# Seven products for thirteen more pairs of row blocks in an fp32 encoder layer

## The chip, the core and the metric

The kernel runs on one core of one Trainium2 chip. The metric is the device time of one execution in microseconds (us). A core has a matrix engine (TensorE, "PE" in the profile, its weight loads "PEld"), VectorE ("DVE"), ScalarE ("ACT"), GpSimd ("POOL") and SyncE ("SP"), which here issues the weight DMAs. Each engine works off its own instructions in order; engines wait for one another by semaphores.

## The reference

One encoder layer on 256 tokens of width 4096, all in float32:

- `h = rms_norm(x)`, then `proj = h @ w_in`, cut into latents for one attention (MLA: 16 heads, with rotary keys), its gate (2048 columns), q, k, v of a second, dilated attention (2048 columns each) and its gate (2048).
- MLA: q from `c_q @ w_uq`, k and v from `c_kv @ w_ukv`, softmax, output; the dilated attention likewise with a distance penalty and three patterns.
- Each output is RMS-normalised and multiplied by `silu(gate)`; then `x = x + concat(y_a, y_b) @ w_out`.
- `x = x + (p @ w_ple) * sigmoid(rms_norm(x) @ w_ple_gate)`, then a last RMS norm.

Nearly all the work is in products of 256 rows with weight matrices of 4096 rows: `w_in`, `w_out` and `w_ple_gate`.

## The kernel before

**Split numbers.** TensorE reads float32 in a rounded form (fp32r). Each operand is therefore cut into a high part (`hi`, rounded by ScalarE, L115 or L829) and a low part (`lo = x - hi`, by VectorE, L116 or L832), and a product is three matmuls (`mm`, L130: L133 hi x hi, L134 the activations' hi x the weights' lo, L135 lo x hi). The activations are split once; every weight tile is split as it arrives.

**Steps.** The kernel is one list `steps`. A step loads a weight tile of 128x1024 (L790, on SP's queue), splits it into a pair of tiles `hi`, `lo`, and runs its matmuls. "Half" below means such a split tile, "lead" the time between the end of its low part and the first matmul that reads it. The main loop (L1430) writes for each step: the loads some steps ahead, the splits some steps ahead (`convert`, as far as tiles are open), the step's matmuls, and then one tick (`advance`, L240) of all running tasks (attention heads, gating, sums). So what lies on VectorE behind what is fixed by this loop, and a split can only be written for a step if the tiles' last user is a step whose matmuls are already written (`tiles`, L1353). The tiles are the ring `WP` of three pairs plus those which a block's `ring` adds from memory that is free then; with one added there are four open, with two five. A ring entry in `gated_rings` (L1194) opens when its flag is set.

**Blocks.** `Block` (L765) multiplies all 256 rows by 1024 columns. It has 32 row blocks of the weights, in 16 pairs. A plain pair ("C" in the strings) takes two steps of four products, that is 2 x 4 x 3 = 24 matmuls of 128x512. A fast pair ("S", `fast_steps`, L808) computes the same 2x2 block product with seven products (Winograd's form of Strassen's scheme): 21 matmuls in four steps of 3, 6, 6 and 6. It needs sums of the activations, made once per pair index by `add_sums` (L848: five operations and a split), and four 128x512 subtractions of weights on VectorE, and its two loads give four split operands of 512, 1024, 1024 and 1024 columns. The seven products lie in eight PSUM banks (m0 to m3, s, o, t0, t1), named by `tags`. When the last fast pair has run, a task (`mid`) combines products; at the block's end another (`done`) adds the rest: in q, k, v these are five operations on L669 (`d_mid`) and four on L687 (`d_done`). The strings in `mix(...)` fix the order; `mix` gives the S the first pair indices.

**Order of the work.** Stage A: the first 1600 columns of `w_in` (400 at a time), while x is transposed. Then "first gates" (block of two latent-gate chunks), then ga2 (third gate chunk) interleaved with `w_uq` and `w_ukv` and the MLA heads (`attend`, L386); `done_uk` (L498) reads the two banks of each `w_ukv` product. Then ga3 (fourth gate chunk), the blocks q0, k0, v0, q1, k1, v1, the four gate chunks of the dilated branch (with its heads), three blocks of `w_out` (o0, o1, o2) and two plain chunks, three blocks of `w_ple_gate` (w0, w1, w2, each with two steps "e" of `w_ple`), and a tail.

**Sums.** `x0_sums` (hook at step 24) serves the first gates, `x_sums` q to v, `y_sums` the `w_out` blocks, and `x1_sums` (spawned six steps into the last plain `w_out` chunk) the `w_ple_gate` blocks. Their results lie in slots such as T0 to T7 and B0 to B7b, which are used again and again by name; a new tile in a slot waits until its last reader is done.

Of the kernel before, what the change touches and what calls it, by code (L numbers as in the profile page):

```python
# [12 lines left out]
F32R = mybir.dt.float32r  # L13
# [5 lines left out]
P = 128  # L19
S = 256  # L20
# [58 lines left out]
def encoder_layer(ctx: ExitStack, tc: tile.TileContext, x, p, positions, g_mix, w_in, g_q_latent, w_uq,  # L79
# [3 lines left out]
    x, p, out = x[0], p[0, 0], out[0]  # L83
    w_in, w_uq, w_ukv, w_out, w_ple, w_ple_gate = (w[0] for w in (w_in, w_uq, w_ukv, w_out, w_ple, w_ple_gate))
# [220 lines left out]
    T7 = {}  # L305

    sums = stat(NT * 6).rearrange("p (c t) -> p c t", t=NT)
# [162 lines left out]
    pairs = {}  # L470
# [58 lines left out]
    us, yT = {}, {}  # L529
# [172 lines left out]
    x1T = {}  # L702
# [49 lines left out]
    WP = ["wp"] * 3  # L752

    class Step:
# [4 lines left out]
        def __init__(self, load, split, run, needs=(), frees=0):  # L759
            self.load, self.split, self.run, self.needs, self.frees, self.after = load, split, run, needs, frees, None  # L760
            self.ring = WP
# [3 lines left out]
    class Block:  # L765
# [6 lines left out]

        NAMES = "M2", "X", "M3", "M4", "M1", "M5", "M6", "M7"

        def __init__(self, w, lhs, sums, name, order, needs, tags, tmp, ring):
            self.w, self.lhs, self.sums, self.name, self.needs, self.tmp = w, lhs, sums, name, needs, tmp
            self.ring, self.tags = ring, dict(zip(self.NAMES, tags))
            self.ps, self.left = {}, {}
            for kind, _ in order:
                for m in ("M1", "M5", "M7", "M6", "M4", "M2", "M3") if kind == "fast" else ("M2", "X", "M3", "M4"):  # L780
                    self.left[m] = self.left.get(m, 0) + (1 if kind == "fast" else 2)
# [66 lines left out]
    def add_sums(n, pair, dst, tmp, name, out, rest=0, first=0):  # L848

        def task():
            def two(op, d, a, b):
                nc.vector.tensor_tensor(d, a, b, op=op)

            if isinstance(tmp, tuple):
                w = [slot(b, [8, P]) for b in tmp]
            else:
                both = slot(tmp, [2, 8, P])
                w = [both[:, 0], both[:, 1]]  # L860
            for j in range(first, n):
# [12 lines left out]
                for _ in range(1 + rest):  # L874
                    yield
        return task()


    y_s, zy = {}, {}
    WIDE_O, FAST_O = 3, 6  # L880
# [7 lines left out]
    def y_sums():  # L888
        while not all(("yT", 0, c) in flags for c in range(FAST_O // 2)):
            yield  # L890
        yield from add_sums(FAST_O, lambda j: [q[:, 2 * (j % 2):2 * (j % 2) + 2] for q in yT[j // 2]], zy_dst, "Al1",
                            "y_sums", y_s)

    def out_mid(k, blk):
        def task():
# [35 lines left out]
    pT, ple, gF, U = [], {}, [], []  # L931
    part2 = [stat(1) for _ in range(NT)]
    blocks = [(512 * c, 512) for c in range(7)] + [(3584, 256), (3840, 256)]
    FAST, WIDE = 6, 3
    zs = {}

    def z_dst(j):
        if j == 0:
            whole = slot("B0", [2, 2 * Q], F32R)
            pT.append(whole[:, 0].rearrange("p (a k t) -> p a k t", a=2, k=2))  # L940
            zs[0] = whole[:, 1].rearrange("p (a i c) -> p a i c", a=2, i=4)
        elif j in (1, 3):
            both = slot(f"B{2 + j // 2}", [2, 2, 4, P], F32R)
            zs[j], zs[j + 1] = both[:, 0], both[:, 1]
        elif j == 5:
            zs[5] = slot("B7a", [2, 4, P], F32R)
            rest = slot("T6", [2, Q])
            P4[1, 0], P4[1, 1] = rest[:, 0], rest[:, 1]
        return zs[j]

    def lhs_x1(kt):
# [173 lines left out]
    M = ("m0", "m1"), ("m2", "m3")  # L1125
# [20 lines left out]
    EVEN, ODD = ("m0", "m1", "s", "o", "m2", "m3", "t0", "t1"), ("m2", "m3", "t0", "t1", "m0", "m1", "s", "o")  # L1146
    LAST = "m2", "m3", "s", "o", "m0", "m1", "t0", "t1"

    def mix(shape):
        n = shape.count("S")  # L1150
        fast, plain_ = iter(range(n)), iter(range(n, 16))
        return [("ple", 0) if x == "e" else ("fast", next(fast)) if x == "S" else ("plain", next(plain_)) for x in shape]

    def lay(blk, order, mid, done, ple=None):
        last = max(i for i, o in enumerate(order) if o[0] == "fast")
        for i, (kind, j) in enumerate(order):
            if kind == "fast":
                new = blk.fast_steps(j)
            elif kind == "ple":
                new = ple  # L1160
            else:
                new = [x for kt in (2 * j, 2 * j + 1) for x in blk.plain_step(kt)]
            if i == last:
                new[-1].after = mid
            if i == len(order) - 1:
                new[-1].after = done
            for x in new:
                x.ring = blk.ring
            steps.extend(new)

    def hook(at, f):
        assert at not in hooks
        hooks[at] = f
# [6 lines left out]
    x0_s, z0 = {}, {}  # L1180

    def z0_dst(j):
        if j < 4:
            if j % 2 == 0:
                both = slot(("B2", "B3")[j // 2], [2, 2, 4, P], F32R)
                z0[j], z0[j + 1] = both[:, 0], both[:, 1]
            return z0[j]
        return slot(f"T{j - 4}", [2, 4, P], F32R)

    def x_pair(j):  # L1190
        return [q[:, 2 * (j % 4):2 * (j % 4) + 2] for q in xT[j // 4]]

    hook(24, lambda: spawn(add_sums(6, x_pair, z0_dst, ("B7a", "B7b"), "x0_sums", x0_s, 2)))
    gated_rings = {("T4", "T7"): ("mid", ("k", 1)), "Al1": ("y_sums", FAST_O - 1), ("T5", "T6"): "kpe"}  # L1194
    order = mix("CCCCSCSCSCSCSCSC")
    blk = Block(w_in[:, OFF_GA:OFF_GA + 1024], lhs_x, x0_s, "x0_sums", order, lambda kt: (), LAST, ("T2", "T3"),
                WP + [("T5", "T6")])
    lay(blk, order, gates_mid(blk), gates_done(blk))
# [7 lines left out]
    hook(len(steps), lambda: spawn(y_stats(0)))  # L1206
    hook(len(steps) + 1, lambda: spawn(x_sums()))
    ga3 = from_x(OFF_GA + 1536, 512, done_gate(0, 3))
    ga3.banks = M[1]
    add(ga3)  # L1210

    x_s = {}
# [10 lines left out]

    for n, key in enumerate((key, i) for i in range(2) for key in "qkv"):
        off = {"q": OFF_Q, "k": OFF_K, "v": OFF_V}[key[0]] + 1024 * key[1]
        order = mix(("CCCCCCCCSCSCSCSC", "CCSCSCSCSCSCSCSC", "CSCSCSCSCSCSCSSC", "CCCCSCSCSCSCSCSC", "CCCCSCSCSCSCSCSC",
                     "CCCCCSCCSCCSCCSC")[n])
        ring = (["B6"], ["B4", "B6"], ["B4", "B6"], ["B4", "B1"], ["B1"], [("T4", "T7")])[n]
        blk = Block(w_in[:, off:off + 1024], lhs_x, x_s, "x_sums", order, lambda kt: (), (EVEN, ODD)[n % 2],
                    "B1" if n < 3 else ("T5", "T6"), WP + ring)  # L1230
        lay(blk, order, d_mid(key, blk), d_done(key, blk))
    beside = [len(steps), len(steps) + 64]
    for c in range(4):
# [6 lines left out]
    for k in range(WIDE_O):  # L1240
        hook(len(steps), only(*(("t0", "t1"), ("m0", "m1"), ("m2", "m3"))[k]))
        for h in range(2):
            hook(len(steps) + 4 + h, lambda c=2 * k + h: load_res(c))
        order = mix(("CCCCCCSCSCSCSCCC", "CCCSCSCSCSCSCSCC", "CCCSCCSCCSCCSCCC")[k])
        blk = Block(w_out[:, 1024 * k:1024 * (k + 1)], lhs_y, y_s, "y_sums", order, lambda kt: need_y(kt // 2),
                    (EVEN, ODD)[k % 2], "Al2" if k < 2 else "Al1", WP + (["Ah2", "Al1"] if k < 2 else [("B7b", "T7")]))
        lay(blk, order, out_mid(k, blk), out_done(k, blk))
# [11 lines left out]
                     lambda j: ["pT"])  # L1259

    for k in range(WIDE):
        order = mix("CCCSCSCSCSCSCSCeC")
        blk = Block(w_ple_gate[:, 1024 * k:1024 * (k + 1)], lhs_x1, x1_s, "x1_sums", [o for o in order if o[0] != "ple"],
                    lambda kt: [("x1T", kt // 4)], LAST, "B6", WP + ["B4", "B5"])
        lay(blk, order, wide_mid(k, blk), wide_done(k, blk), wide_ple(k))
    wide_end = len(steps)
    hooks[wide_end + 2] = lambda: (load_g(0), load_g(1), spawn(late_gains()))
# [2 lines left out]
    for c, (lo, n) in enumerate(blocks):  # L1270
        if c < 2 * WIDE:
            continue
        w, per = cols(w_ple_gate, lo, n), 1024 // n
# [156 lines left out]
    for i, step in enumerate(steps):  # L1430
# [23 lines left out]
        n = 0  # L1454
# [33 lines left out]
```

## Time and profile before

| | us |
|---|---|
| median of 3 runs (lowest, highest) | 1938.94 (1937.89, 1939.36) |
| the profiled execution, whole | 1939.64 |
| its span, first to last instruction | 1937.7 |
| DVE `lo` of 128x1024 (L116), mean of one | 1.223 |
| ACT `hi` of 128x1024 (L115), mean of one | 1.060 |
| DVE subtraction of 128x512 (L816), mean of one | 0.690 |
| load of 512 KB of `w_in`, issue to landing, median | 4.0 |

The profile is one execution. Its first lines give each engine's busy time; the chain is the work that ended last, followed back; "L133 <- DVE B L119" means that the instruction of line 133 waited until VectorE's instruction of line 119 that writes a tile B was done. A matmul's duration in a row is pipelined, so the rate is read from starts, not from durations. A table by stretches has, per row, the stretch, its length, busy time of PE, PEld, DVE, ACT and POOL with the number of instructions in brackets, the granted TensorE clock as a share of the full one, the DMA engines' busy share and GB/s. A timeline row has start, duration, engine, line, operation, `out<-in`, shapes, and in square brackets the idle time before it and who ended it.

### The profile page before, as it was taken

The page shows a single profiled execution, that of the slowest core. Times are in us where ns is not written, and L with a number is a line of the kernel's source. Part 1 is how long each engine was busy: PE and PEld are TensorE (multiplying, and loading weights), DVE is VectorE, ACT ScalarE, POOL GpSimd, SP SyncE. Part 2 cuts the span into 40 slices and gives each one's busy share as a digit, 9 for nine tenths or more (in the row PEclk, how much of TensorE's full clock was granted, in tenths as well). Part 3 has the DMA queues.
Part 4 walks back from the last instruction along what each step waited for, and adds up shares of the span by engine and source line. Part 5 has one row for each costly group of instructions (what it writes and reads, how often), then busy time and mean ns, then how long its engine had stood idle before and what let it go on. Part 6 is the DMA issues. An engine that isn't in the chain of part 4 may idle for free.

```text
span 1937.7 us, 25517 instructions
## 1 busy us (share of the span) xinstructions
PE 1919.8 (99%) x9314; PEld 1636.6 (84%) x9314; DVE 1497.8 (77%) x2071; ACT 1082.0 (56%) x1482; POOL 72.1 (4%) x124
## 2 busy tenths in 40 slices
PE   9999999999999999999999999999999999999997
PEld 8998889997888888888888888888888888888887
DVE  7767966665889988878677777888876598888765
ACT  6555565564555555545456676556555455655543
POOL 1001011110000000000000010000000000000000
PEclk9999999999999999999999999999999999999999
DMA  7666655444656566666654446665666556566655
GB/s 251 190 184 196 196 170 149 145 146 148 188 177 211 196 217 197 216 191 200 215 189 143 149 152 217 220 215 176 205 194 212 187 187 218 191 218 206 225 185 178
DMA packets 146477, 370.58 MB, mean 191 GB/s; under 512 B 11924, under 2 KB 45808, under 8 KB 146096
## 3 DMA queue, kind: packets, MB, share of 16 engines
q1 hardware_dynamic: 144432, 361.80, 58.5%
q0 software_dynamic: 1920, 7.15, 1.1%
q8 instruction: 73, 1.20, 0.2%
q14 instruction: 52, 0.43, 0.1%
HBM read 364.72 MB, written 4.19 MB: 190 GB/s over the span
## 4 chain that ended last, share of the span: by engine, by line
PE 95%; DVE 3%; ACT 1%; issue 1%; DMA 1%; SPq 0%; DVEq 0%; ACTq 0%
PE m L134 20%; PE m L133 20%; PE m L135 20%; PE t L133 4%; PE t L135 4%; PE t L134 4%; PE o L134 3%; PE o L135 3%; PE o L133 3%; PE s L134 3%; PE s L133 3%; PE s L135 3%; DVE lo L116 1%; PE t L443 1%; PE t L393 0%
## 5 line engine op out<-in xcount | busy, mean ns | idle before, releaser
L116 DVE TENSOR_TENSOR lo<-raw,hi 128x1024 fp32r<-128x1024 f32 (+4 forms) x503 | 560.3, 1122 | 239.4 <-ACT hi L115 238.0
L115 ACT ACTIVATE hi<-raw 128x1024 fp32r<-128x1024 f32 (+4 forms) x503 | 488.1, 979 | 333.1 <-PE m L135 137.8
L133 PE MATMUL m<-hi,Ah 128*128 128x512 f32 (+2 forms) x1122 | 426.9, 381 | 2.7 <-DVE B L119 2.7
L134 PE MATMUL m<-lo,Ah 128*128 128x512 f32 (+2 forms) x1122 | 421.7, 376 | 1.0 <-DVE lo L832 0.5
L135 PE MATMUL m<-hi,Al 128*128 128x512 f32 (+2 forms) x1118 | 419.1, 375 | 0.0
L133 PEld LDWEIGHTS m<-hi,Ah 128*128 128x128 f32 x1122 | 211.8, 189 | 32.8 <-issue 3.3
L134 PEld LDWEIGHTS m<-lo,Ah 128*128 128x128 f32 x1122 | 211.9, 189 | 32.6 <-DVE lo L116 2.2
L135 PEld LDWEIGHTS m<-hi,Al 128*128 128x128 f32 x1118 | 211.0, 189 | 32.9 <-DVE Al L127 0.2
L133 PE MATMUL m<-hi,B 128*128 128x512 f32 (+1 forms) x405 | 154.6, 382 | 0.0
L135 PE MATMUL m<-hi,B 128*128 128x512 f32 (+1 forms) x405 | 150.9, 373 | 0.0
L134 PE MATMUL m<-lo,B 128*128 128x512 f32 (+1 forms) x405 | 150.8, 372 | 0.0
L116 DVE TENSOR_TENSOR B<-raw,B 128x1024 fp32r<-128x1024 f32 (+1 forms) x72 | 79.6, 1118 | 26.3 <-ACT B L115 26.3
L115 ACT ACTIVATE B<-raw 128x1024 fp32r<-128x1024 f32 (+1 forms) x72 | 69.2, 975 | 44.6 <-PE o L135 15.6
L135 PEld LDWEIGHTS m<-hi,B 128*128 128x128 f32 x405 | 76.0, 188 | 11.2
L134 PEld LDWEIGHTS m<-lo,B 128*128 128x128 f32 x405 | 76.2, 188 | 10.2 <-DVE lo L116 0.2
L133 PEld LDWEIGHTS m<-hi,B 128*128 128x128 f32 x405 | 76.1, 188 | 10.0
L116 DVE TENSOR_TENSOR T<-t,T 128x512 fp32r<-128x512 f32 (+1 forms) x65 | 44.5, 685 | 41.7 <-ACT T L115 41.4
L829 ACT ACTIVATE hi<-raw 128x1024 fp32r<-128x1024 f32 x45 | 47.9, 1064 | 44.2 <-PE o L135 17.6
L115 ACT ACTIVATE hi<-B 128x1024 fp32r<-128x1024 f32 x42 | 44.7, 1064 | 41.2 <-PE o L135 28.1
L115 ACT ACTIVATE hi<-T 128x1024 fp32r<-128x1024 f32 x34 | 36.2, 1063 | 52.6 <-PE o L135 28.6
L133 PE MATMUL m<-B,Ah 128*128 128x512 f32 (+1 forms) x174 | 64.5, 371 | 0.0
L135 PE MATMUL m<-B,Al 128*128 128x512 f32 (+1 forms) x174 | 64.3, 370 | 0.0
(751 smaller groups left out, 3827.6 us busy)
## 6 DMA issues: line engine op xcount, KB each, us to landing
raw<-in_w_in_dram SPq DMA_DIRECT2D x320, 512.0 KB, 4.0
raw<-in_w_out_dram SPq DMA_DIRECT2D x128, 512.0 KB, 4.4
raw<-in_w_ple_gate_dram SPq DMA_DIRECT2D x128, 512.0 KB, 4.6
raw<-in_w_in_dram SPq DMA_DIRECT2D x63, 400.0 KB, 3.2
raw<-in_w_uq_dram SPq DMA_DIRECT2D x32, 384.0 KB, 3.4
raw<-in_w_ukv_dram SPq DMA_DIRECT2D x16, 512.0 KB, 4.1
T<-in_x_dram SPq DMA_DIRECT2D x7, 512.0 KB, 5.8
T<-in_x_dram POOLq DMA_DIRECT2D x7, 512.0 KB, 8.0
```

What stands on the lines that cost most here:

```text
L115: nc.scalar.activation(hi, src, AF.Copy)
L116: nc.vector.tensor_tensor(lo, src, plain(hi), op=ALU.subtract)
L133: nc.tensor.matmul(ps, ah, bh, start=start, stop=False)
L134: nc.tensor.matmul(ps, ah, bl, start=False, stop=False)
L135: nc.tensor.matmul(ps, al, bh, start=False, stop=stop)
L443: nc.tensor.transpose(tp[:, k, t * P:(t + 1) * P], e[:, t, k * P:(k + 1) * P], ident)
L829: nc.scalar.activation(hi, r[1], AF.Copy)
```

## The change

Three things change.

1. **More fast pairs**, 86 in place of 73: first gates 6 to 7; k0 7 to 8; q1 and k1 6 to 8; v1 4 to 6 (pair indices 0 to 3, 6 and 7, as T4 and T7 become split tiles in this block); o1 6 to 7; o2 4 to 6; w1 and w2 6 to 7. q0 (4), v0 (8), o0 (4) and w0 (6) stay. Strings move with it: k0, q1 and k1 now have v0's "CSCSCSCSCSCSCSSC".
2. **What the sums need.** x0, y and x1 sums are made for seven pairs instead of six. The seventh x0 sum takes B7a (the sums' scratch moves to T2, T3), the seventh y sum T4, the seventh x1 sum B5, which leaves the ring of the `w_ple_gate` blocks. Because q1 to v1 use pairs 6 and 7, T5 and T6 hold sums there, so the subtractions' scratch is B1, and B1 leaves the rings of q1 and k1. In k1 the last four entries of the string ("CSSC") use `WP` alone (`spare`), since B4 receives k1's result.
3. **Banks.** ga3 takes m0, m1 in place of m2, m3; q0 and k0 get other bank orders to fit.

```
-        yield from add_sums(FAST_O, lambda j: [...yT[j // 2]], zy_dst, "Al1", "y_sums", y_s)
+        pair = lambda j: [q[:, 2 * (j % 2):2 * (j % 2) + 2] for q in yT[j // 2]]
+        yield from add_sums(FAST_O, pair, zy_dst, "Al1", "y_sums", y_s)
+        while ("yT", 1, 3) not in flags:
+            yield
+        yield from add_sums(FAST_O + 1, pair, lambda j: slot("T4", [2, 4, P], F32R), ("T7", "B7b"), "y_sums", y_s, first=FAST_O)
...
-    FAST, WIDE = 6, 3
+    FAST, WIDE = 7, 3
...
+        elif j == 6:
+            zs[6] = slot("B5", [2, 4, P], F32R)
...
-    def mix(shape):
-        n = shape.count("S")
-        fast, plain_ = iter(range(n)), iter(range(n, 16))
+    def mix(shape, pairs=range(16)):
+
+        chosen = list(pairs)[:shape.count("S")]
+        fast, plain_ = iter(chosen), iter(j for j in range(16) if j not in chosen)
...
-                x.ring = blk.ring
+                x.ring = blk.ring if i < len(order) - blk.spare else WP
...
-        return slot(f"T{j - 4}", [2, 4, P], F32R)
+        return slot(("T0", "T1", "B7a")[j - 4], [2, 4, P], F32R)
...
-    hook(24, lambda: spawn(add_sums(6, x_pair, z0_dst, ("B7a", "B7b"), "x0_sums", x0_s, 2)))
+    hook(24, lambda: spawn(add_sums(7, x_pair, z0_dst, ("T2", "T3"), "x0_sums", x0_s, 2)))
...
-    order = mix("CCCCSCSCSCSCSCSC")
+    order = mix("CCSCSCSCSCSCSCSC")
...
-    ga3.banks = M[1]
+    ga3.banks = M[0]
...
-        order = mix(("CCCCCCCCSCSCSCSC", "CCSCSCSCSCSCSCSC", "CSCSCSCSCSCSCSSC", "CCCCSCSCSCSCSCSC", "CCCCSCSCSCSCSCSC",
-                     "CCCCCSCCSCCSCCSC")[n])
-        ring = (["B6"], ["B4", "B6"], ["B4", "B6"], ["B4", "B1"], ["B1"], [("T4", "T7")])[n]
-        blk = Block(w_in[:, off:off + 1024], lhs_x, x_s, "x_sums", order, lambda kt: (), (EVEN, ODD)[n % 2],
-                    "B1" if n < 3 else ("T5", "T6"), WP + ring)
+        full = "CSCSCSCSCSCSCSSC"
+        order = mix("CCCCCCCCSCSCSCSC") if n == 0 else mix(full) if n < 5 else mix("CCCCSCSCSCSCSCSC", (0, 1, 2, 3, 6, 7))
+        ring = (["B6"], ["B4", "B6"], ["B4", "B6"], ["B4"], ["B4"], [("T4", "T7")])[n]
+        tags = LAST if n == 0 else ("t0", "t1", "m2", "m3", "m0", "m1", "s", "o") if n == 1 else (EVEN, ODD)[n % 2]
+        blk = Block(w_in[:, off:off + 1024], lhs_x, x_s, "x_sums", order, lambda kt: (), tags, "B1", WP + ring,
+                    4 if n == 4 else 0)
...
-        order = mix(("CCCCCCSCSCSCSCCC", "CCCSCSCSCSCSCSCC", "CCCSCCSCCSCCSCCC")[k])
+        order = mix(("CCCCCCSCSCSCSCCC", "CCSCSCSCSCSCSSCC", "CCCSCSCSCSCSCSCC")[k])
...
-        order = mix("CCCSCSCSCSCSCSCeC")
+        order = mix("CCCSCSCSCSCSCSCeC" if k == 0 else "CCSCSCSCSCSCSSCeC")
...
-                    lambda kt: [("x1T", kt // 4)], LAST, "B6", WP + ["B4", "B5"])
+                    lambda kt: [("x1T", kt // 4)], LAST, "B6", WP + ["B4"])
```

More of the change, by code (lines that the diff above doesn't have):

```diff
@@ L773, in encoder_layer, with __init__ @@
         NAMES = "M2", "X", "M3", "M4", "M1", "M5", "M6", "M7"
-        def __init__(self, w, lhs, sums, name, order, needs, tags, tmp, ring):
+        def __init__(self, w, lhs, sums, name, order, needs, tags, tmp, ring, spare=0):
             self.w, self.lhs, self.sums, self.name, self.needs, self.tmp = w, lhs, sums, name, needs, tmp
+            self.spare = spare
             self.ring, self.tags = ring, dict(zip(self.NAMES, tags))
@@ L890, in y_sums @@
             yield
-        yield from add_sums(FAST_O, lambda j: [q[:, 2 * (j % 2):2 * (j % 2) + 2] for q in yT[j // 2]], zy_dst, "Al1",
-                            "y_sums", y_s)
+        pair = lambda j: [q[:, 2 * (j % 2):2 * (j % 2) + 2] for q in yT[j // 2]]
[3 more added lines that the diff above has]
+        yield from add_sums(FAST_O + 1, pair, lambda j: slot("T4", [2, 4, P], F32R), ("T7", "B7b"), "y_sums", y_s, first=FAST_O)
     def out_mid(k, blk):
```

## The prediction

> **What bounds the kernel now.** I read the busy shares first, then the chain that ended last, TensorE's waits, the table by stretches (one per block of products), and last the timeline around the places that change.
>
> ```profile
> PE 1919.8 (99%) x9314; PEld 1636.6 (84%) x9314; DVE 1497.8 (77%) x2071; ACT 1082.0 (56%) x1482; POOL 72.1 (4%) x124
> ...
> PE 95%; DVE 3%; ACT 1%; issue 1%; DMA 1%; SPq 0%; DVEq 0%; ACTq 0%
> ```
>
> TensorE is the bound: it is 95% of the chain, so a matmul less is worth its start-to-start time unless something else is then late. That time comes from a block without gaps: k1 (832.39 to 915.35 us) issues 366 matmuls of 512 columns in 82.96 us, 0.227 us each; the row's 0.39 us is pipelined latency. A plain pair (24 matmuls) takes 5.44 us, a pair by seven products (21) 4.76. VectorE is what could be late. Back to back its operations start 1.135 us apart (128x1024) and 0.602 us apart (128x512). A plain pair costs it two of the first, 2.27 us; a seven-product pair four subtractions, one short and three long low halves, 6.41 us: 1.65 us more than TensorE's 4.76.
>
> ```profile
> 667.80:749.40 81.60, 81.60 (x361) 67.59 (x360) 76.16 (x89) 47.98 (x50) 0.00 (x0) 1.00 0.64 206
> 749.40:832.40 83.00, 83.00 (x368) 68.72 (x367) 69.31 (x78) 43.40 (x45) 0.00 (x0) 1.00 0.63 203
> 832.40:915.30 82.90, 82.90 (x367) 68.70 (x366) 67.56 (x77) 45.30 (x47) 0.00 (x0) 1.00 0.61 197
> ```
>
> These stretches are v0 (eight fast pairs), q1 and k1 (six each); the columns are stretch, PE, PEld, DVE, ACT and POOL busy, clock, DMA. Eight pairs fill VectorE to 93% and TensorE has no gap. So capacity suffices on the average, and the question is the lead: how long a low half is finished (L116, L832) before the first matmul that reads it (L134).
>
> **What goes.** 13 pairs change, three matmuls each: 39 x 0.227 = **8.85 us less**. Weight bytes and the number of their DMAs stay the same; POOL gets nothing new.
>
> **ga3 in other banks.** Between ukv and ga3 TensorE stands still for m2 and m3, which done_uk(7) still reads:
>
> ```profile
> PE m L133 <- DVE B L119: 2.7, 2, 2.2
> ```
>
> ```profile
> 440.00:442.40 2.40, 0.28 (x3) 0.04 (x1) 1.86 (x4) 0.47 (x1) 0.00 (x0) 1.00 0.24 32
> 442.40:444.00 1.60, 1.06 (x4) 0.64 (x5) 1.05 (x3) 1.26 (x3) 0.00 (x0) 1.00 0.75 284
> 444.00:447.60 3.60, 3.60 (x10) 2.77 (x11) 2.94 (x6) 1.13 (x2) 0.00 (x0) 0.53 0.11 15
> ```
>
> The timeline has 2.35 us lost at 442.5, 0.65 at 443.9, and then matmuls 0.427 us apart at clock 0.53, 1.77 us: 4.77 in all. m0 and m1 are read for the last time by 437.0 (L592), so ga3 starts at 440.1. Late next is the head behind its first step: its product needs the split that VectorE ends at 444.4, behind done_uk's ping-pong with ScalarE, while TensorE is there at 442.8: 1.7 us. I take **3.05 us less**; ends 1.3 (the clock drops again) and 4.8 (no wait).
>
> **Two fast pairs in a row ("SS").** In v0, with five tile pairs for the halves, the lead falls from 3.57 us at a pair's fourth half (ended 734.52, read at 738.09) to 1.22 at the next one's second (738.91, read at 740.13): 2.35 us.
>
> ```profile
> 735.76 0.68 DVE L116 TENSOR_TENSOR lo<-raw,hi 128x512 fp32r<-128x512 f32 x1
> 736.37 1.41 DVE L816 TENSOR_TENSOR B<-raw,B 128x512 f32<-128x512 f32 x2
> 737.69 1.22 DVE L832 TENSOR_TENSOR lo<-raw,hi 128x1024 fp32r<-128x1024 f32 x1
> ...
> 744.50 2.19 DVE L669 SCALAR_TENSOR_TENSOR B<-t,st,B 128x512 f32<-128x512 f32 x3
> ```
>
> With four tile pairs, as in k1 now, a half waits for its tile (below, 1.30 us idle) and the fourth has a lead of only 1.06 (907.72, read at 908.77):
>
> ```profile
> 906.49 1.23 DVE L116 TENSOR_TENSOR lo<-T,hi 128x1024 fp32r<-128x1024 f32 x1 [1.30 <-ACT hi L115]
> ...
> 913.33 2.35 DVE L116 TENSOR_TENSOR lo<-raw,hi 128x1024 fp32r<-128x1024 f32 x2
> 915.59 1.41 DVE L687 SCALAR_TENSOR_TENSOR B<-m,st,B 128x512 f32<-128x512 f32 x2
> ```
>
> 1.06 - 2.35 = -1.3: TensorE waits **1.3 us**. So in q1 (ring now B4 alone), w1 and w2 (B5 is gone from the ring): **3.9 us**. o1 keeps five and its lead stays at 1.2: nothing.
>
> **Blocks that begin with "CS".** After a block's last fast pair VectorE has five sums (L669, 3.3 us), at its end four more (L687, 2.64). In v0, the only block that begins so, the second half of the first fast pair has a lead of 0.25 (673.92, read at 674.16). After a block that ends in "SSC" VectorE is 0.52 later (the second half of the next block has a lead of 3.23 in q1, 3.75 in v0): 0.3 us of wait for v0, and for q1, whose first tiles still lie five apart: **0.6**. With four tiles I put a fast pair where v1 has its second plain one: halves end at 915.68, plus 2.64 sums, 1.81 and 2.34 for the pair's first two steps, 922.46, read at 921.69: **0.8 us** for k0 behind q0, and 0.8 + 0.5 = **1.3** for k1 behind q1. k0's own banks m2 and m3 are free in time (d_done reads them first, by 587.2; needed at 586.9 and 587.6).
>
> **The end of k1, three tiles.** The spare puts its last C, S, S, C on WP. A half then starts when the step three before it ends, and ends 2.5 us after that (2.45 in the three-tile rows at 168 us). From the start of that first C: its end is 5.44, S1's 6.12. S3's half ends at 7.95, read at 7.71: 0.25 late. The next S1 ends at 10.9 (read 10.7): 0.25. Its S2 needs four subtractions' worth more, 13.25 (read 11.6): 1.65. Then d_mid takes 16.85 to 20.15, and the last plain half, now behind it, ends at 21.3 (read 20.05): 1.25. Together **3.4 us**. v1 begins with four plain pairs and recovers. Ends 1.3 (one SS) and 4.
>
> **w0 start.** The seventh sum (five operations 1570.37 to 1572.02 for the sixth, then a 0.60 split: 2.25 us) comes two steps after the sixth, in front of the first fast pair, whose leads are already 0.42, 0.19, 0.05 and 0.06 us (1581 to 1586). Nothing hides it: **2.25 us**; ends 1 and 2.5. The x0 and y sums lie where VectorE is idle a third (stage A, 68% busy) or the lead is 5 us and more (o0 at 1244 to 1250): nothing; without that cover 2.25 each.
>
> **First gates.** One fast pair moves ahead to 168.4, 4.14 us more VectorE work before the tight place at 190 (0.68 us lost). VectorE is idle 1.2 to 1.5 us before each of the five halves from 161 to 172, 7 us, but only three tiles are open there, so the idle time can't be used freely, and done_a's small operations (some 0.2 us each, 178.9 to 192.1) come with the steps. Walked half by half from 168.4 with those durations, TensorE waits 0.4 us (plain pair at 174), 0.55, 0.4, 0.95 (the fast pair from 180), 0.3 and 0.2: 2.8 against 1.2 lost in this block now. **1.6 us**; ends 0 (all of it finds idle time) and 4.1 (none).
>
> **Sum.** Less: 8.85 + 3.05 = 11.9. More: 1.6 + 0.8 + 0.6 + 1.3 + 1.3 + 3.4 + 2.25 + 2.6 = 13.85 (q1, then w1 and w2 of the 3.9). Net 1.95 us more. The profiled execution took 1939.64 us around its span of 1937.7; that gives 1941.6. The median shown, 1938.94, lies 0.7 lower: **1941 us**, no change by the 0.2% (3.9 us) that a measurement here can tell.
>
> **Rivals.**
> A, the lead is regained (chance 0.2): ScalarE and VectorE start halves earlier than the walks say, and only half the waits are left, 6.9 us: 1938.9 - 11.9 + 6.9 = 1934; with none left 1927. For it: v0 shows eight pairs without a gap. Against: four-tile leads of 1.06 us recur pair after pair in k1.
> B, slower (0.18): TensorE's new gaps drop its clock, as at 444. Each costs 1.7 us (the 1.77 above). The place is the end of k1 with gaps of 1.65 and 1.25 close together: 1942.7; if each gap of 1.2 us and more does it (k1 start, q1, w0, w1, w2, k1 twice), 7 x 1.7 = 12: 1953. It decides between 0.68 us, after which the clock stayed 1.00 (191 to 197), and the 2.35 and 0.65 that tripped it. In the Trainium skill, "TensorE: Matmul & The Clock Gate", section "Why this matters for your kernels", idle gaps up to about 3 us are harmless; by that rule B gives nothing and 1941 stands, but the row at 444 speaks against the rule, since gaps of 2.35 and 0.65 us with matmuls between them were enough.
> C, VectorE falls further behind (0.12): k0 to k1 now ask it for 8 x 6.41 + 8 x 2.27 + 5.94 = 75.4 us in 81.6, four times in a row, and one 2 us delay in each is passed on: 4 x 2 = 8 more, 1949. Against: 6 us of idle in each block.
>
> My forecast gets 0.5, with its own range 1937 to 1945. The range runs from A's half to B's middle: **1934 to 1947**. Faster 0.18 (A), same 0.48 (0.36 of mine, the rest edges of the rivals), slower 0.34 (0.14 of mine, 0.10 B, 0.10 C).
>
> **What would show it.** Matmuls 9314 - 39 = 9275. No wait on L119 before ga3, clock 1.00 behind it. New waits of TensorE on DVE lo L116 or L832, at most 2 us each: in q1, at k1's start, most at its end, w0's start, w1, w2; none in v1, o1, o2. If L116 and L832 stay at 0.8 us in total, the walks are wrong and A holds; a PEclk under 1 outside the tail is B.

## The result, and the profile after

The changed kernel takes **1949.01 us** (median of 5 runs, 1947.32 to 1950.29) against 1938.94 (5 runs, 1937.89 to 1939.36): ratio 1.0052, 95% interval 1.0037 to 1.0067. It is slower, where I had forecast 1941 and no change. The profiled execution of after took 1950.29 us with a span of 1948.4, which is 10.7 more than before's 1937.7. In the changed kernel the lines from L775 on stand lower: L833 is before's L832 (low half of a seven-product pair), L817 its L816 (weight subtraction), L904 its L900, L924 its L920.

Page of the profile after, busy shares and the chain that ended last:

```profile
PE 1916.1 (98%) x9275; PEld 1628.2 (84%) x9275; DVE 1556.9 (80%) x2167; ACT 1102.7 (57%) x1511; POOL 71.5 (4%) x124
...
PE 83%; DVE 11%; issue 2%; DMA 2%; ACT 1%; SPq 0%; DVEq 0%; ACTq 0%
```

The 39 matmuls are gone (9314 to 9275), but PE's share of the chain fell from 95% to 83% and DVE's rose from 3% to 11%. What TensorE waits for, in after (engine, its matmul, who released it: sum, times, longest):

```profile
PE m L134 <- DVE lo L833: 6.1, 6, 2.0
PE m L134 <- DVE B L833: 2.7, 2, 1.5
PE m L134 <- DVE lo L116: 2.3, 6, 1.3
...
PE m L730 <- DVE T L924: 1.2, 1, 1.2
...
PE m L133 <- ACT Al L115: 0.8, 1, 0.8
```

The first three are low halves that come too late, as forecast. The last two were not forecast: they lie at the start of o2 (1393.2 us) and in o1's first fast pair (1319.5 us). The table by stretches of after, at the places shown of before (ga3's start, then v0, q1, k1):

```profile
441.00:444.00 3.00, 3.00 (x15) 2.14 (x12) 2.12 (x4) 0.78 (x2) 0.00 (x0) 1.00 0.32 60
444.00:447.60 3.60, 2.55 (x16) 2.17 (x16) 3.32 (x7) 3.60 (x8) 0.00 (x0) 1.00 0.28 103
666.00:748.10 82.10, 81.94 (x362) 67.56 (x361) 76.73 (x90) 46.40 (x49) 0.00 (x0) 1.00 0.65 205
748.10:831.70 83.60, 82.25 (x362) 67.49 (x361) 75.89 (x89) 47.51 (x50) 0.00 (x0) 1.00 0.62 195
831.70:919.00 87.30, 83.09 (x362) 67.23 (x361) 78.19 (x92) 47.90 (x50) 0.00 (x0) 1.00 0.61 192
```

ga3 starts without a stop, two waits of 0.87 and 0.50 us remain one step later, and the clock stays at 1.00. k1 has six matmuls less than before and is 4.3 us longer.

Block lengths from the first matmul of each to that of the next, in us, with the time lost to the blocks' waits and clock drops (change of length plus 0.68 per pair changed) beside the loss that was predicted:

| block | before | after | change | lost | predicted |
|---|---|---|---|---|---|
| first gates | 85.3 | 86.2 | +0.9 | 1.6 | 1.6 |
| ga2 with uq, ukv; ga3 | 254.4 | 251.1 | -3.3 | -3.3 | -3.05 |
| k0 | 82.3 | 82.7 | +0.4 | 1.1 | 0.8 |
| v0 | 81.6 | 82.0 | +0.4 | 0.4 | 0.3 |
| q1 | 83.0 | 83.6 | +0.6 | 1.9 | 1.6 |
| k1 | 83.0 | 87.3 | +4.3 | 5.7 | 4.7 |
| v1 | 84.3 | 83.0 | -1.3 | 0.0 | 0 |
| o1 | 84.9 | 85.3 | +0.4 | 1.0 | 0 |
| o2 | 86.3 | 86.4 | +0.1 | 1.4 | 0 |
| w0 | 90.1 | 93.3 | +3.2 | 3.2 | 2.25 |
| w1 | 88.4 | 89.7 | +1.3 | 2.0 | 1.3 |
| w2 | 88.4 | 92.0 | +3.6 | 4.3 | 1.3 |

Stage A is 0.2 longer; all other blocks are the same to 0.1. Of the 8.8 us by which the losses exceed the predicted ones (22.6 without the banks, against 13.85), 2.4 lie in o1 and o2, 3.0 in w2, 0.9 in w0, 1.0 in k1, 0.7 in w1.

**Two clock drops.** Table by stretches of after, around w0's and w2's longest gaps (seventh value from the left: the granted clock):

```profile
1584.00:1586.90 2.90, 0.94 (x4) 0.64 (x4) 2.80 (x7) 1.80 (x2) 0.00 (x0) 0.99 0.49 167
1586.90:1590.30 3.40, 3.40 (x10) 2.62 (x9) 3.30 (x7) 1.26 (x2) 0.00 (x0) 0.50 0.52 154
1817.30:1818.97 1.67, 0.18 (x2) 0.10 (x1) 1.67 (x3) 1.18 (x2) 0.00 (x0) 1.00 0.78 221
1818.97:1822.38 3.41, 3.41 (x9) 2.65 (x10) 3.25 (x3) 1.87 (x3) 0.00 (x0) 0.50 0.57 196
```

After a gap of 2.12 us in w0, and one of 1.66 in w2, the clock is 0.50 for 3.4 us: matmuls start 0.427 us apart, eight in a time in which fifteen fit.

### The profile page after: what moved, and what is told of

It reads as the page before. It is cut to its first block, busy times and chain, and to the rows that moved or that the text cites. A ratio compares the mean times of both kernels' runs of the same rounds, so it can differ in the third digit from the quotient of the medians.

```text
span 1948.4 us, 25587 instructions
## 1 busy us (share of the span) xinstructions
PE 1916.1 (98%) x9275; PEld 1628.2 (84%) x9275; DVE 1556.9 (80%) x2167; ACT 1102.7 (57%) x1511; POOL 71.5 (4%) x124
## 4 chain that ended last, share of the span: by engine, by line
PE 83%; DVE 11%; issue 2%; DMA 2%; ACT 1%; SPq 0%; DVEq 0%; ACTq 0%
PE m L134 18%; PE m L135 18%; PE m L133 18%; PE o L134 3%; PE o L135 3%; PE o L133 3%; PE s L134 3%; DVE lo L116 3%; PE s L133 3%; PE s L135 3%; PE t L134 3%; PE t L135 3%; PE t L133 3%; DVE B L817 2%; DVE B L116 1%
## 5 line engine op out<-in xcount | busy, mean ns | idle before, releaser
L116 DVE TENSOR_TENSOR lo<-raw,hi 128x1024 fp32r<-128x1024 f32 (+3 forms) x507 | 557.8, 1108 | 206.1 <-ACT hi L115 205.7
L115 ACT ACTIVATE hi<-raw 128x1024 fp32r<-128x1024 f32 (+3 forms) x507 | 485.6, 965 | 290.2 <-PE m L135 152.5
L115 ACT ACTIVATE hi<-B 128x1024 fp32r<-128x1024 f32 x90 | 95.4, 1061 | 122.6 <-PE o L135 65.6
L133 PE MATMUL m<-hi,B 128*128 128x512 f32 (+1 forms) x425 | 163.0, 384 | 0.0
L135 PE MATMUL m<-hi,B 128*128 128x512 f32 (+1 forms) x425 | 159.2, 375 | 0.0
L116 DVE TENSOR_TENSOR lo<-B,hi 128x1024 fp32r<-128x1024 f32 x90 | 108.6, 1221 | 34.6 <-ACT hi L115 34.6
L830 ACT ACTIVATE hi<-raw 128x1024 fp32r<-128x1024 f32 x57 | 60.6, 1064 | 55.4 <-PE o L135 30.4
L817 DVE TENSOR_TENSOR B<-raw,B 128x512 f32<-128x512 f32 x124 | 85.5, 689 | 2.2
L116 DVE TENSOR_TENSOR B<-raw,B 128x1024 fp32r<-128x1024 f32 (+1 forms) x58 | 63.6, 1101 | 10.7 <-ACT B L115 10.7
L833 DVE TENSOR_TENSOR lo<-raw,hi 128x1024 fp32r<-128x1024 f32 x57 | 69.5, 1219 | 3.0 <-ACT hi L830 3.0
L115 ACT ACTIVATE B<-raw 128x1024 fp32r<-128x1024 f32 (+1 forms) x58 | 55.4, 960 | 27.0 <-PE o L135 11.2
```

The lines of the kernel that those rows point to most:

```text
L115: nc.scalar.activation(hi, src, AF.Copy)
L116: nc.vector.tensor_tensor(lo, src, plain(hi), op=ALU.subtract)
L133: nc.tensor.matmul(ps, ah, bh, start=start, stop=False)
L135: nc.tensor.matmul(ps, al, bh, start=False, stop=stop)
L817: nc.vector.tensor_tensor(dst, a, b, op=ALU.subtract)
L830: nc.scalar.activation(hi, r[1], AF.Copy)
```

## Theories

Mine: the pairs saved are repaid in TensorE's waits on halves, and these are made by tiles and by lead, place by place, not by VectorE's load. What the prediction lacked was (1) a wait at o1's start, since its first fast pair now runs into the read of a bank; (2) POOL's loads: two move to a tight place, because the slots that they fill are freed later, and one stands where it stood, but two fast pairs in a row now lie beside it; (3) clock drops after the two longest gaps. Rivals: VectorE's whole load is the limit, so that a wait taken away in one place comes back in the next (the prediction's C); or the clock drops alone carry the excess.

## Experiments

### The banks alone

```
-    ga3.banks = M[1]
+    ga3.banks = M[0]
...
+        tags = LAST if n == 0 else ("t0", "t1", "m2", "m3", "m0", "m1", "s", "o") if n == 1 else (EVEN, ODD)[n % 2]
```

This is the kernel before with these lines, `tags` taking the place of the old order.

> The kernel before with one part of the change alone: the fourth latent gate chunk in the banks m0 and m1, and the order of banks in q0 and k0 that follows from it; all numbers of fast pairs as before. Theory (the prediction's term for the banks is right: after shows its wait of 1.3 us and the clock drop behind it gone, 3.3 us less over ga2 and ga3): time 1935 to 1936.5, ga2 and ga3 together 251 in place of 254.4 us, no clock drop at 444 us, q0 and k0 unchanged to 0.5 us. Rival (VectorE is a fixed amount late there and the wait only moves into ga3's end or q0): time 1937.6 to 1939, a wait of 1 to 2 us in ga3's second half or in q0's first three tiles.

Measured: 1936.66 us against 1938.36, ratio 0.9993 (0.9984 to 1.0002): too small to tell from no change by the times. The blocks tell it: ga2 and ga3 together take 251.3 us in place of 254.4, there is no clock drop, and q0 is unchanged. But k0 is 0.9 longer, where at most 0.5 was expected, with a wait of 0.82 us on `d_done`'s first read (L687). It appears here and not in after: here the read stands behind two halves which end 1.4 us after q0's last matmul, in after 0.3 us. So the term for the banks holds, and a part of it goes again where k0 begins with two plain pairs.

### The last three blocks as before

```
-    FAST, WIDE = 7, 3
+    FAST, WIDE = 6, 3
...
-        order = mix("CCCSCSCSCSCSCSCeC" if k == 0 else "CCSCSCSCSCSCSSCeC")
+        order = mix("CCCSCSCSCSCSCSCeC")
...
-                    lambda kt: [("x1T", kt // 4)], LAST, "B6", WP + ["B4"])
+                    lambda kt: [("x1T", kt // 4)], LAST, "B6", WP + ["B4", "B5"])
```

> The changed kernel with its last stage as before: six embedding-gate pairs in w0 to w2, their order of steps of before, tiles B4 and B5 in the ring of the loads; the rest is as changed. Theory (the stage is a loss of 8.1 us: 2.1 + 0.4 + 1.35 + 0.3 + 1.9 us of waits on VectorE's halves, and two clock drops of 1.7 us, against 2.7 us of matmuls saved): 1941 us, w0, w1, w2 at 90.1, 88.4 and 88.4 us, no stretch at granted clock 0.5 after the first 300 us. Prediction's own sizes (no clock drop, shorter waits): 1945.5 us. Rival (the waits come from VectorE's total lateness, carried over from the stages ahead): w0 still has its wait near 1586 us and the time stays above 1946 us.

Measured: 1941.89 us, ratio to before 1.0018 (1.0010 to 1.0027); w0, w1, w2 at 89.7, 88.4 and 88.4 us and no clock drop. Some 7 of the 10 us came from these three blocks, and nothing of it is carried in from the blocks ahead.

### Two fast pairs in a row, on five tiles and on four

Both have six pairs in w1 and w2, the last two in a row ("CCCCSCSCSCSCSSCeC"), and no seventh sum; one has B4 and B5 in the ring, the other B4 alone.

> The changed kernel with six embedding-gate pairs, the seventh sum and its use of B5 taken out, tiles B4 and B5 both in the ring (five tiles), and in w1 and w2 a string that still ends its fast pairs with two in a row (CCCCSCSCSCSCSSCeC). Theory (a wait at two fast pairs in a row is a matter of tiles: the second pair's first half needs the tile that the first pair's last part has just freed, and a fifth tile uncouples them): no wait of over 0.3 us at the two in a row, w1 and w2 at 88.4 us each, time 1941. Rival (VectorE's pace: the two pairs in a row need 6.9 us of halves in 6.1 us of matmuls whatever the tiles): a wait of 0.8 us or more there in both, w1 and w2 at 89.2 us or more, time 1942.5 or more.

> The same as the run with five tiles, but only B4 in the ring (four tiles). Theory (tiles): a wait of 1.35 us at the two fast pairs in a row in w1 and in w2; in w2 0.3 to 0.6 us more where the 1 MB load of the final gain lies beside it, and a clock drop behind it if the two add up to 1.9 us or more: w1 89.7, w2 90 to 92 us. Its w0 shows four tiles without the seventh sum: 0.5 to 1.2 us of wait near 1586 us and no clock drop if the sum was the larger part, 2 us and a drop if the ring alone was. Rival (VectorE's pace): the waits are the same as with five tiles, and w0 as in the kernel before.

Measured: 1941.33 and 1946.15 us (one run each). With five tiles, table by stretches over w1 and w2 (the second and third value are the length and PE's busy time):

```profile
1655.10:1743.50 88.40, 88.40 (x391) 73.20 (x390) 75.67 (x87) 53.08 (x63) 0.00 (x0) 1.00 0.62 202
1743.50:1831.90 88.40, 88.40 (x391) 73.20 (x390) 76.04 (x87) 52.73 (x63) 1.11 (x2) 1.00 0.68 229
```

With four, TensorE's waits over w1 and w2:

```profile
PE m L134 <- DVE lo L833: 1.2, 1, 1.2
PE m L134 <- DVE B L833: 1.2, 1, 1.2
```

The same VectorE work in the same order: no gap with five tiles, and one gap of 1.35 us from start to start in each block with four. The rival of VectorE's pace falls; the price of two fast pairs in a row is that of the missing tile. w0 on four tiles without the seventh sum has 0.3 us of wait and no drop, so its 2.1 us are the sum's. The w2 with four tiles had 1.35 and not more: its 1 MB load of the final gain (POOL, L968) is issued at 1813.87 us, after the weight loads of both pairs (the last of them at about 1809).

### The order of o1's pairs: the residual loads

```
-        order = mix((...)[k])
+        order = mix((...)[k], (6, 0, 1, 2, 3, 4, 5) if k == 1 else range(16))
```

> The changed kernel with one edit: in o1 the fast pairs come in the order 6, 0, 1, ... 5, so that the tile T4 of the seventh y sum is read first and given back some 60 us earlier; sums, order of steps and counts are as changed. Theory (the residual loads of x that take T4 and T5 move: in the kernel before POOL issues them at 1241 us, in after at 1378 us, and there they share the DMA engines with the raw w_out loads, which then land 6 to 7.9 us after their issue, so that o1's last adds and, behind them, o2's start come late): POOL's issue of x1[4] lies 40 us or more earlier, the wait of 1.4 to 1.7 us at the start of o2 is gone or below 0.3 us, o2 at 85.0 to 85.3 us, the time 1.4 us less. Rival (VectorE is late at o2's start because of the two fast pairs in a row at o1's end, wherever the loads lie): the loads move and the wait stays within 0.3 us of 1.4.

The rows of the timeline for POOL's load of x1[4] and x1[5], in the kernel before,

```profile
1241.10 1.45 POOL L713 DMA_DIRECT2D T<-in_x_dram  x2 [66.65 <-DVE B L116]
```

in after, where the slot T4 holds the seventh y sum until o1's last fast pair,

```profile
1377.87 1.44 POOL L713 DMA_DIRECT2D T<-in_x_dram  x2 [201.23 <-PE s L135]
```

and with this order of pairs:

```profile
1321.72 1.44 POOL L713 DMA_DIRECT2D T<-in_x_dram  x2 [145.46 <-PE s L135]
```

Timeline of after behind that load, the end of o1 and the start of o2:

```profile
1384.36 1.07 ACT L115 ACTIVATE hi<-raw 128x1024 fp32r<-128x1024 f32 x1 [2.89 <-DMA raw<-in_w_out_dram]
...
1387.78 1.22 DVE L116 TENSOR_TENSOR lo<-raw,hi 128x1024 fp32r<-128x1024 f32 x1 [0.77 <-ACT hi L115]
...
1389.50 1.23 DVE L116 TENSOR_TENSOR T<-raw,B7b 128x1024 fp32r<-128x1024 f32 x1 [0.50 <-ACT B7b L115]
...
1391.84 1.28 DVE L924 TENSOR_TENSOR T<-T,t 128x512 f32<-128x512 f32 x2
...
1393.18 0.55 PE L730 MATMUL m<-ident,T 128*128 128x128 f32 x3 [1.22 <-DVE T L924]
```

ScalarE waits 2.89 us for a weight tile, then 1.26 and 0.66 for the next two (weight loads there land 5.6 us after issue in the median and 7.9 at most). VectorE idles 0.77 and 0.50 us for the halves of the last two, and `out_done`'s adds (L924), behind these halves, come 1.2 us too late for the transposes of x1. With the load moved, the loads land at most 5.8 us after issue, VectorE idles 0.44 us there, the wait at o2's start is 0.46 us in place of 1.38, o2 takes 85.4 in place of 86.4, and the run 1946.22 us (one run). So the load was two thirds of it; 0.46 stays, a little more than expected, and comes from the same adds behind the same halves.

A late tile alone is not enough. In the run with k1's fourth tile (below) the load lies where after has it (issued at 1375.92 us), a weight load takes 8.8 us and ScalarE waits 3.88 us for its tile, yet o2 takes only 85.6 us. There VectorE's order at that place is another: no half stands between `out_mid`'s last sums (L904) and the adds, where after has three. In the five other runs that keep o1's string and order and the load, o2 takes 86.3 to 86.8 us. So the loss is the load's together with the halves that stand ahead of the adds.

### The order of w2's pairs: the load of the final gain

```
-        order = mix(...)
+        order = mix(..., (0, 1, 2, 5, 6, 3, 4) if k == 2 else range(16))
```

> The changed kernel with one edit: in w2 the fast pairs come in the order 0, 1, 2, 5, 6, 3, 4, so that the sums 3 and 4, whose tile B3 the second 1 MB load of the final gain takes, are read last, and this load is issued behind the two fast pairs in a row. Theory (the load lies beside the four raw loads of the two pairs and makes their tiles late by 0.3 to 0.6 us on top of the 1.35 us that four tiles cost there; the sum of 1.9 us is enough for a clock drop of 1.7 us): w2's wait back to 1.35 us, no stretch at granted clock 0.5 behind it, w2 89.4 to 89.9 us in place of 92.0, the time 2.2 to 2.6 us less. Rival (the wait in w2 is longer because VectorE is later there anyway): 1.9 us and the drop stay.

Measured: w2's long wait is 1.35 us in place of 1.66 with 0.25 ahead of it, no drop follows, and w2 takes 89.8 us in place of 92.0: the block did as expected. The run's time did not (1949.14 us, one run), because a drop came in k1 instead, where the same gap of 1.67 us had had none in after. In the two runs below that leave o1's order alone and have this load beside the two pairs (the late sum, and k1's tiles) w2's wait is 1.65 and 1.67; in the run with o1's later start it is 1.35 although the load lies there, since the weight tile landed 0.7 us less late (ScalarE waited 1.44 us for it in place of 2.14). So the load costs 0.3 us, and none where the tile lands 0.7 us earlier, by one run.

### k1's end with a fourth tile

```
-                    4 if n == 4 else 0)
+                    1 if n == 4 else 0)
```

> The changed kernel with one number changed: in k1 only the last item, not the last four, is kept to three tiles. Theory (the prediction's step for k1's end: three tiles couple VectorE's halves to the matmuls that free the tiles, and the waits of 0.35 + 0.2 + 1.66 + 1.46 us there are tiles' waits; with the fourth tile back the two pairs in a row cost the 1.35 us that they cost in q1): k1's end at 1.4 to 2.2 us of waits, k1 85.2 to 85.8 us in place of 87.3, the time 1.5 to 2.1 us less, or the fourth tile's later release costs something in v1 (0 to 1 us). Rival (VectorE's load is what binds in k1): the waits stay at 3.2 us or more in all.

Measured: k1's end has two waits, 1.35 and 1.46 us, in place of four with 3.7 in all; k1 takes 86.2 us, more than the 85.8 expected, and v1 is unchanged; 1945.54 us (one run). Of the 3.5 us by which the run is faster than after's median, only 1.1 are k1's: in its profile w2 has no clock drop and o2 is 0.7 shorter. The waits lie between the two: three tiles cost the 0.35, the 0.2 and 0.3 of the 1.66; the last 1.46 stays, because the last plain pair still has three tiles (the next experiments).

### The parts without waits, together

The change without its seventh pairs in the gates, o1, w1 and w2, with k0 as before, in k1 the last entry alone on `WP` (`spare` 1), and:

```
-        order = mix("CCCCCCCCSCSCSCSC") if n == 0 else mix(full) if n < 5 else mix("CCCCSCSCSCSCSCSC", (0, 1, 2, 3, 6, 7))
+        order = mix(("CCCCCCCCSCSCSCSC", "CCSCSCSCSCSCSCSC", "CSCSCSCSCSCSCSSC", "CCSCSCSCSCSCSCSC", "CCSCSCSCSCSCSCSC",
+                     "CCCCSCSCSCSCSCSC")[n], (0, 1, 2, 3, 6, 7) if n == 5 else range(16))
```

> Of the change only the parts that the walks through the tiles leave without waits: the fourth latent gate chunk's banks, seven fast pairs in q1 and k1 (with two plain pairs at the start and one between every two fast), six in v1, six in o2; latent gates, k0, v0, o1, the y and x1 sums and w0 to w2 are as before. Theory (waits come only where two fast pairs follow each other on four tiles, or where a stage starts on a fast pair with no lead): 1936.6 of the run with the banks alone, less 3 pairs of 0.68 us in q1, k1 and o2 and two in v1: 3.4 us, so 1932 to 1934. Rival 1 (VectorE's total load is the limit, a pair saved there is given back at the next boundary): 1935.5 or more. Rival 2 (four tiles alone are too few for q1 and k1, whatever the order): waits of 0.5 us or more in the middle of q1 or k1, 1934.5 to 1937.

Measured: **1933.75 us**, ratio 0.9977 (0.9968 to 0.9986). q1 82.3, v1 83.0 and o2 85.0 us without a wait; k1 83.9 with one of 1.46. (o2 gains two pairs, so the expected sum was 4.1 us, not 3.4; the wait in k1 takes 1.5 of it.) VectorE's work rose by 23 us against before and nothing came back at a next boundary: rival 1 falls. Four tiles suffice with a plain pair between fast ones. The timeline of this kernel at k1's end:

```profile
905.63 2.19 DVE L669 SCALAR_TENSOR_TENSOR B<-t,st,B 128x512 f32<-128x512 f32 x3
907.74 1.40 DVE L669 SCALAR_TENSOR_TENSOR B<-m,st,B 128x512 f32<-128x512 f32 x2
909.05 2.35 DVE L116 TENSOR_TENSOR lo<-raw,hi 128x1024 fp32r<-128x1024 f32 x2
```

With three tiles, the last plain half can only be written behind the five sums of `d_mid` (L669); its matmul was due at 908.86 and came at 910.33.

### k1's end, two ways

From the chosen parts, k1 as "CSCSCSCSCSCSCSCC", or with six pairs as "CCSCSCSCSCSCSCCC" (and `spare` 2):

> The kernel of the chosen parts with k1's seven fast pairs moved one plain pair ahead (CSCSCSCSCSCSCSCC). Theory (the wait of 1.46 us at k1's end there is its last plain pair on three tiles behind the five combining operations of the fast products; with one more plain pair between, the fourth tile is still in the ring behind these operations): the wait at k1's end is gone, at its start 0.3 to 0.9 us appear, for the fast pair there comes with little lead; k1 82.6 to 83.2 us in place of 83.9, the time 1932.5 to 1933.3. Rival (the combining operations themselves, 3.6 us of VectorE, are what is waited for): the 1.46 us stay and the start's wait comes on top, 1934.2 or more.

> The kernel of the chosen parts with six fast pairs in k1 in place of seven (CCSCSCSCSCSCSCCC, the last two items on three tiles). Theory (as in the run before this): the 1.46 us at k1's end go, one pair of 0.68 us comes back: k1 83.0 to 83.3 us, the time 1932.8 to 1933.4. Rival (three tiles cost their wait wherever they begin): 1.0 us or more stays at k1's end, k1 84.1 us or more, 1934 or more.

Measured: 1932.87 us, ratio 0.9977 (0.9968 to 0.9987), and **1932.58 us**, 0.9973 (0.9963 to 0.9983). In both the 1.46 us are gone. The first has 0.94 at k1's start (k1 83.35, a little over the 83.2 expected), the second none (82.96). They can't be told apart by time; both are faster than the kernel before by some 5 us.

### The seventh x1 sum later

```
-        return add_sums(FAST, ...)
+        pair = lambda j: [q[:, 2 * (j % 4):2 * (j % 4) + 2] for q in x1T[j // 4]]
+        yield from add_sums(FAST - 1, pair, z_dst, "B1", "x1_sums", x1_s)
+        for _ in range(14):
+            yield
+        yield from add_sums(FAST, pair, z_dst, "B1", "x1_sums", x1_s, first=FAST - 1)
```

> The changed kernel with one edit: the seventh x1 sum is formed 14 steps later, in the middle of w0, where the halves lead the matmuls by 1 to 3 us, and not just ahead of w0's first fast pair, where they lead by 0.1 to 0.3 us. Theory (w0's gap of 2.0 to 2.1 us is this sum's VectorE work laid into a place without lead; four tiles alone cost 0.3 us there): the gap near 1585 us is 0.3 to 0.6 us, no clock drop in w0, w0 89.9 to 90.3 us in place of 92.3 (without a drop) to 93.3; the seventh pair in w1 and w2 is as in after. Rival (the seventh sum costs its time wherever it lies, since VectorE has no slack in w0): a gap or gaps of 1.5 us or more later in w0.

Measured: w0's gap is 0.31 us, there is no drop, w0 takes 89.9 us in place of 93.3; 1947.16 us (one run). Same work, 14 steps later: free.

### o1's first fast pair later

```
-        order = mix(("CCCCCCSCSCSCSCCC", "CCSCSCSCSCSCSSCC", "CCCSCSCSCSCSCSCC")[k])
+        order = mix(("CCCCCCSCSCSCSCCC", "CCCSCSCSCSSCSSCC", "CCCSCSCSCSCSCSCC")[k])
```

> The changed kernel with one edit: o1 keeps its seven fast pairs, but begins one plain pair later and puts two fast pairs in a row twice at its end (CCCSCSCSCSSCSSCC). Theory (the wait of 0.93 us in o1's first fast pair, which the prediction missed, comes from the bank m1: the transposed x1 pieces of o0 are read out of it until then, and the first pair that begins 5.4 us earlier runs into that; o1's five tiles carry two pairs in a row without a wait): no wait of over 0.2 us in o1, o1 84.2 to 84.5 us in place of 85.3. Rival (VectorE is late at o1's start by its load, wherever the pair lies): a wait of 0.5 us or more stays, or appears at the first of the two pairs in a row.

Measured: no wait in o1, which takes 84.26 us in place of 85.3; but o2's start loses 0.95 and 1.68 us in place of 1.38 (two fast pairs in a row now lie nearer to it, beside the moved load), and w0 again has a drop after a gap of 1.97: 1947.59 us (one run). So the wait of 0.93 belongs to the early start, and two pairs in a row on five tiles cost nothing within the block. The rows of after's timeline at that place:

```profile
1318.48 0.87 DVE L127 SCALAR_TENSOR_TENSOR Al<-m,gT,Ah 128x256 fp32r<-128x256 f32 x2
1318.88 0.62 ACT L115 ACTIVATE Al<-raw 128x512 fp32r<-128x512 f32 x1
...
1319.50 0.47 PE L133 MATMUL m<-hi,Ah 128*128 128x512 f32 x1 [0.76 <-ACT Al L115]
```

The matmul of the pair's third step is the first to write m1, which the transposed pieces of o0's x1 are read from (L127) until 1319.35. The profile names ScalarE's Al, which ends at 1319.50 but is a half for a later step; I take the bank for the cause. In the run with o1's other order of pairs this matmul reads another sum and waits the same 0.93 us, again until 0.15 us after L127's end, which speaks for the bank; that it is the bank and not another effect of the earlier start was not tried apart.

### What the clock does after a gap

w0's gap in the run with o1's other order of pairs, against after's rows above:

```profile
1582.65:1584.80 2.15, 0.21 (x1) 0.00 (x0) 2.12 (x4) 1.05 (x2) 0.00 (x0) 1.00 0.64 213
1584.80:1588.20 3.40, 3.26 (x12) 2.10 (x12) 3.23 (x10) 2.33 (x4) 0.00 (x0) 1.00 0.49 154
```

The same gap (2.13 us), and the clock stays at 1.00. Over the 14 profiled executions, from the end of stage A to the start of the tail: after gaps of 0.68 to 1.57 us the clock never dropped (96 gaps); after 1.65 to 1.67 in 2 of 12; after 1.97 to 2.23 in 4 of 6. One drop added 1.0 us to w0 (93.3 against 92.35), 1.8 to w2 (92.0 against 90.2) and 1.5 to k1 (88.8 against 87.35): near the prediction's 1.77, and less where the waits behind it get shorter by it.

**Where the gap lies.** The traces also record when the granted clock changed. In each of the 14 executions all changes lie on whole multiples of 3.413 us from the first record, which itself comes 4.1 to 10.7 us after the first instruction. So cut each execution along this grid. The stretch of after that ends where w0's drop begins holds the whole gap:

```profile
1583.45:1586.87 3.42, 1.46 (x7) 0.91 (x6) 3.28 (x9) 1.77 (x2) 0.00 (x0) 1.00 0.51 153
```

In the run with o1's other order the grid cuts the gap (1582.70 to 1584.83 us) at 1583.44, and TensorE is busier in both stretches:

```profile
1580.03:1583.44 3.41, 2.83 (x13) 2.02 (x11) 3.31 (x9) 1.06 (x1) 0.00 (x0) 1.00 0.31 73
1583.44:1586.86 3.42, 2.03 (x8) 1.44 (x9) 3.26 (x9) 2.58 (x3) 0.00 (x0) 1.00 0.46 146
```

Now add up TensorE's idle time in each stretch: what lies beyond 0.227 us from one start to the next, or beyond 0.11 us behind a transpose of 128 columns, the pace of these matmuls back to back. After's stretch above has 2.23 us of it, the fuller one of the other run 1.72. All six stretches with a drop behind them have 2.02 to 2.48 us, and none of the others, over 6,800, has more than 1.99. So a drop follows when about 2.0 us of one stretch of 3.413 are idle, an estimate from these counts. It fits that a gap of 1.66 us tripped the clock in w2 of after, where 0.25 and 0.11 us of other waits lie in the same stretch, and that in the kernel before, at ga3's start, the second gap of 0.65 us counted too: the grid leaves only 1.67 of the first gap's 2.23 us in that stretch. All this is read from the traces afterwards; no run moved a gap on purpose.

## Why the prediction was wrong

Right: the 39 matmuls; the banks (3.1 to 3.4 us, 3.05 forecast; 1.4 us of waits remain one step later, 1.7 forecast); k0, v0 and q1 (each 0.15 to 0.35 over); k1's start (1.35 measured, 1.3) and end (3.7 in all, 3.4), with the waits at the places named; two pairs in a row on four tiles (1.35 wherever that wait stood alone, 1.3 forecast); v1 without a wait; o1's five tiles. There the walks half by half are good to some 0.35 us.

Right by luck: the first gates. They lose the 1.6 us forecast, but not as walked. The walk had 0.4 us at 174 and most of the rest in the fast pair from 180. In after the first fast pair waits 1.46 us, by the profile for a bank that VectorE still reads (not tried apart), and at 185.2 us there are 0.47:

```profile
172.98 0.41 DVE L116 TENSOR_TENSOR T<-t,T 128x256 fp32r<-128x256 f32 x1
173.44 0.50 PE L133 MATMUL t<-hi,B 128*128 128x512 f32 x1 [1.30 <-DVE T L116]
```

The steps that failed; together they make the losses 22.6 us where the sum has 13.85:

- **"POOL gets nothing new."** The instructions are the same, but two of POOL's loads wait for slots which new sums hold, and some 135 us later they share the DMA engines with o1's last weight loads. With "none in v1, o1, o2" o2's 1.4 us were put at nothing; moving the load back took 0.9 of it away.
- **"o1 keeps five and its lead stays at 1.2: nothing."** That is right for its two pairs in a row and wrong for its start, which now comes one plain pair earlier: 0.93 us. I had not asked which bank the first fast pair writes, and who still reads it; the same question was missed in the first gates.
- **The start of w1 and w2** was not walked: their first fast pair also comes a plain pair earlier, 0.34 us each.
- **w0 and w2, the sizes, and with them rival B.** w0's sum cost 2.1 us, as worked out (2.25), and then a clock drop; in w2 the 1.35 grew to 1.66 by the load of the final gain, a few tenths stood ahead of it, and a drop followed. Rival B was there with 0.18, but its place was put at k1's end, and it priced single gaps where idle time within one stretch of 3.413 us decides. The drops came at w0 and w2 in after, and at k1 in another run. The forecast treated them as a case of their own, where they should have been a term: the five profiled executions with w0's gap had 2, 0, 1, 1 and 1 drops, at 1.0 to 1.8 us each.
- **Rival C** (VectorE as a whole falls behind) would have given the measured 1949, but for the wrong reason: no loss is handed on. Each that was tried goes, wholly or for the most part, when its own tile, place or load is mended, and 23 us of VectorE work more in the chosen parts cost nothing.

By the Trainium skill, "TensorE: Matmul & The Clock Gate", section "Why this matters for your kernels", idle gaps up to about 3 us are harmless. These runs don't agree: drops came after 1.65 to 1.67 us in 2 of 12 gaps and after 1.97 to 2.23 us in 4 of 6. The same page, "What's actually happening", has the clock follow a free-running activity window of about 3.4 us. These traces agree: the clock changes on a grid of 3.413 us, and one and the same gap trips it or not by where it falls on the grid.

Open: how much idle time in a stretch is the exact limit; whether the bank m1 alone makes o1's wait; and the 0.46 us that stay at o2's start.

## What to carry to other kernels

When a slot gets a longer-lived tenant, look up who is next in it: a load that waits for the slot on another queue moves with it, and may land where weight loads are needed on time. A step that the tighter engine has room for on the average is free where its lead is 1 us and more and costs its whole length where the lead is nothing, so put extra work, and two heavy steps in a row, by the lead at that place and by the tiles open there. A clock drop is not priced by the longest gap alone: add up the idle time that can fall into one stretch of 3.4 us. Of a set of like edits, take those whose walk shows no wait: five pairs and the banks gave 5 us, all thirteen lost 10.

## What the hardware showed unexpectedly

TensorE's granted clock drops to 0.50 for 3.41 us on a grid of 3.413 us whose place differs from execution to execution: in six of six cases the stretch ahead of the drop had 2.02 us or more of idle time. So it dropped after a gap of 1.66 us that had other waits beside it, and stayed up after one of 2.13 that the grid cut in two. A megabyte loaded by POOL beside the weight stream took single weight loads of 512 KB from 4.5 us (median) to 7.9 us (o1, two loads of 512 KB) and 9.2 us (w2, one of 1 MB) from issue to landing, and ScalarE waited 2.9 us for such a tile in after, 4.0 in the run with o1's later start.
